# First projection of a two-layer decoder trunk: fewer column sums, unused matmuls between the input loads, a fixed order of TensorE, VectorE and ScalarE, and the state-space parameters behind it

## The chip, the cores and the metric

One core of one Trainium2 chip runs the whole kernel. The metric is the device time of one execution in microseconds (us); below 1 us the text uses the same unit (0.23 us). TensorE (PE) multiplies matrices, VectorE (DVE) and ScalarE (ACT) do elementwise work, GpSimd (POOL) a few small things, and SyncE (SP) issues nearly all the transfers (DMAs). Each engine works through its own list of instructions in order and waits where an operand is not there.

## The reference, cut to what matters

The trunk has two layers; x is 512 tokens by 1024 channels, kept transposed (channels on partitions). Only the start of layer 0 is touched:

```
c_act = silu(c)
mod   = c_act @ ada_w[0] + ada_b[0]           # shift, scale, gate
h     = rms_norm(x, norm_w[0]) * (1 + scale) + shift
u, z  = split(h @ s5_w_in, 2)                 # first projection: 1024 -> 4096 columns
dt = exp(log_dt); mag = exp(lam_re*dt); ab = mag*(cos, sin)(lam_im*dt); q = ...   # state-space parameters
y  = diagonal complex recurrence over u, in chunks of 128 tokens
```

`rms_norm` needs for each token the sum of x*x over 1024 channels, then the power -1/2 of its mean.

## The kernel before

All large products are made of three matmuls on values split in two parts (`fp32r` high part and the rest): high weight by high x, high weight by low x, low weight by high x (`mm3`). A weight tile `wraw` (128x1024) is loaded, ACT copies it to `whi`, DVE subtracts to get `wlo`.

**Before the first matmul.** SP loads c, then x in four loads of two tiles each (`x_sb`), biases, norm weights, constants `cst`, then for k = 0 two tiles of the modulation weights (`adaw`, columns k and 8+k) and one weight tile. PE spreads c over the partitions (L271) and ACT takes its silu (`cact`). ACT squares the eight x tiles, DVE adds them in pairs, and PE sums each pair over the partitions (`col_sums`, L120: four matmuls with one moving column each, sixteen in all) into `pc`. DVE scales `pc` and adds eps, POOL takes the power -1/2 (L129), PE spreads the result over all partitions (`rstd_row`, L134) into `pb`, ACT copies it to `rs`.

**The first projection, u half A (L300 on).** For k = 0..7: two weighted row sums on DVE (`ada_acc`, L103) give shift and scale of 128 channels, two small adds and one small multiply finish them (`ada_fix`, `scale_cols`: `mods`, `acol`). `norm_tile` (L138 to L142) multiplies x by rstd on DVE (`nt`), ACT writes the high part `hhi` and the full value `nh`, DVE subtracts (`hlo`). Then 24 matmuls add into eight accumulators `acc` in PSUM. These 192 matmuls are 'the projection' below. Nothing but a scheduler with priorities sets the order of the engines here.

**After it.** The other 24 column blocks of the projection come as units of 24 matmuls (`unit`, tile `ps_mm`): they fill PE while the recurrence runs. `s5_params` computes the parameters, mostly 128x128 steps on DVE with three kinds of table functions on ACT, and stores powers to DRAM (`wd`). `s5_load` fetches them back (`wt`), with `bB` and the projected `U`; `s5_bl` multiplies on DVE, `s5_mask` on ACT gives `bl`, and `s5_v` multiplies U by bl on PE (`ps_v`, L514). From the first `ps_v` on, sixteen steps of the recurrence run in an order that is written out by hand for PE and DVE; a step begins on DVE with `s5_rot` (`za`, L523), which reads `ps_v`.

Of the kernel before, what the change touches and what calls it, by code (L numbers as in the profile page):

```python
# [41 lines left out]
def hybrid_kernel(ctx: ExitStack, tc: tile.TileContext, a, out, dbg=None):  # L42
# [27 lines left out]
    eps_c, hpi_c, rnd_c = cols[:, 0:1], cols[:, 1:2], cols[:, 2:3]  # L70

# [183 lines left out]
    with tc.tile_pool(name="xa", bufs=1, side="right") as xa, tc.tile_pool(name="psA", bufs=1, space=PSUM) as psA:  # L255
# [10 lines left out]
        SY.dma_start(cst, a["cst"])  # L266
# [3 lines left out]
        for q in range(2):  # L270
            TE.matmul(acc[q], one_row, crow[:, q * T:(q + 1) * T], start=True, stop=True)  # L271
            S.activation(out=cact[:, q * T:(q + 1) * T], in_=acc[q], func=AF.Silu)
# [4 lines left out]
        def mod_cols(k, aw0, aw1, raw):  # L277
            mod_cols.last = ada_acc(k, aw0)
            ada_acc(8 + k, aw1)
            ada_fix(k, 1)  # L280
            ada_fix(8 + k, 1)
            scale_cols(0, k)
            return split_w(raw)

        ld0 = loads(0)

        with tc.high_priority():
            sqs = []
# [10 lines left out]
        for k in range(KT):  # L299
            whi, wlo = mod_cols(k, *loads(k)) if k else w0  # L300
            norm_tile(x_sb[:, k, :], rs if k else pb, acol[:, k:k + 1], mods[:, k:k + 1], hhi[:, k, :], hlo[:, k, :], xa)
            if k == 0:
                acc += [psA.tile([P, T], F32, tag=f"acc{m}", name=f"acc{m}") for m in (6, 7)]
            for m in range(8):
                mm3(acc[m], whi[:, m * P:(m + 1) * P], wlo[:, m * P:(m + 1) * P], hhi[:, k, :], hlo[:, k, :],
                    k == 0, k == KT - 1)
# [1062 lines left out]
```

## Time and profile before

| | |
|---|---|
| runs | 1084.86 us median of 3 (1084.2 to 1087.56) |
| the profiled execution | 1086.08 us, of which the span from first to last instruction is 1084.4 us |
| busy over the span | PE 96%, DVE 71%, ACT 55%, POOL 5% |
| mean granted TensorE clock | 0.992 of full |

Engine busy shares are means over stages with different limits. The rows that matter are those of the first 110 us: when each engine starts a step, how long it takes, and what it waited for before. In a row of the timeline the first number is the start, the second how long the (merged) work lasted, the brackets give the idle time before it and what ended that.

### The profile page before, as it was taken

The page shows a single profiled execution, that of the slowest core. Times are in us where ns is not written, and L with a number is a line of the kernel's source. Part 1 is how long each engine was busy: PE and PEld are TensorE (multiplying, and loading weights), DVE is VectorE, ACT ScalarE, POOL GpSimd, SP SyncE. Part 2 cuts the span into 40 slices and gives each one's busy share as a digit, 9 for nine tenths or more (in the row PEclk, how much of TensorE's full clock was granted, in tenths as well). Part 3 has the DMA queues.
Part 4 walks back from the last instruction along what each step waited for, and adds up shares of the span by engine and source line. Part 5 has one row for each costly group of instructions (what it writes and reads, how often), then busy time and mean ns, then how long its engine had stood idle before and what let it go on. Part 6 is the DMA issues. An engine that isn't in the chain of part 4 may idle for free. (4 is left out here: it accounts for less than half of the span.)

```text
span 1084.4 us, 15225 instructions
## 1 busy us (share of the span) xinstructions
PE 1041.8 (96%) x5620; PEld 869.5 (80%) x5620; DVE 774.9 (71%) x1246; ACT 599.8 (55%) x1163; POOL 57.5 (5%) x62
## 2 busy tenths in 40 slices
PE   7999999998999989999999999999999999999997
PEld 5887878886888868878899777778888888887887
DVE  5994999998999838666785688679951444556253
ACT  4573799989787564334446566733343655424241
POOL 0100000000000000000001004310020000200000
PEclk9999999998999999999999999999999999999999
DMA  8776666675354268866751342132241001123342
GB/s 300 265 244 200 192 195 197 190 214 168 99 148 126 91 248 313 299 208 225 251 179 57 111 164 78 59 99 96 104 131 60 20 20 39 59 72 110 100 146 78
DMA packets 85628, 161.42 MB, mean 149 GB/s; under 512 B 10417, under 2 KB 44593, under 8 KB 85554
## 3 DMA queue, kind: packets, MB, share of 16 engines
q1 hardware_dynamic: 84546, 157.31, 45.0%
q0 software_dynamic: 1008, 3.15, 1.1%
q8 instruction: 44, 0.72, 0.3%
q14 instruction: 30, 0.25, 0.1%
HBM read 141.67 MB, written 18.74 MB: 148 GB/s over the span
## 5 line engine op out<-in xcount | busy, mean ns | idle before, releaser
L79 ACT CAST whi<-wraw 128x1024 fp32r<-128x1024 f32 (+1 forms) x101 | 99.1, 981 | 175.8 <-PE ps_mm L93 74.9
L80 DVE TENSOR_TENSOR wlo<-wraw,whi 128x1024 fp32r<-128x1024 f32 (+1 forms) x101 | 116.1, 1149 | 92.9 <-ACT whi L79 79.6
L92 PE MATMUL ps_mm<-g_hhi,whi 128*128 128x512 f32 x360 | 148.3, 412 | 0.4 <-ACT whi L79 0.4
L93 PE MATMUL ps_mm<-g_hlo,whi 128*128 128x512 f32 x360 | 147.0, 408 | 0.0
L94 PE MATMUL ps_mm<-g_hhi,wlo 128*128 128x512 f32 x360 | 145.8, 405 | 0.5 <-DVE wlo L80 0.5
L94 PEld LDWEIGHTS ps_mm<-g_hhi,wlo 128*128 128x128 f32 x360 | 67.7, 188 | 14.7 <-DVE wlo L80 1.0
L92 PE MATMUL ps_mm<-hhi,whi 128*128 128x512 f32 x192 | 79.3, 413 | 0.0
L92 PEld LDWEIGHTS ps_mm<-g_hhi,whi 128*128 128x128 f32 x360 | 67.7, 188 | 14.3 <-ACT whi L79 0.8
L93 PEld LDWEIGHTS ps_mm<-g_hlo,whi 128*128 128x128 f32 x360 | 67.8, 188 | 12.6
L94 PE MATMUL ps_mm<-hhi,wlo 128*128 128x512 f32 x192 | 75.8, 395 | 0.0
L93 PE MATMUL ps_mm<-hlo,whi 128*128 128x512 f32 x192 | 75.5, 393 | 0.0
L857 DVE SCALAR_TENSOR_TENSOR ac<-ps_mm,cw,ac 128x509 f32<-128x509 f32 (+2 forms) x87 | 64.7, 744 | 3.6 <-ACT ac L854 2.9
L103 DVE SCALAR_TENSOR_TENSOR adaw<-adaw,cact 128x1024 f32<-128x1024 f32 x48 | 58.8, 1228 | 5.0 <-DMA adaw<-in_adaw_dram 4.9
L92 PE MATMUL ps_gh<-yAhi,whi 128*128 128x512 f32 x128 | 53.8, 420 | 3.6 <-ACT yAhi L79 3.6
L346 DVE TENSOR_TENSOR wlo<-wraw,whi 128x1024 fp32r<-128x1024 f32 x40 | 48.7, 1219 | 10.8 <-ACT whi L340 10.8
L340 ACT CAST whi<-wraw 128x1024 fp32r<-128x1024 f32 x40 | 41.8, 1044 | 24.2 <-issue 7.7
L93 PE MATMUL ps_gh<-yAlo,whi 128*128 128x512 f32 x128 | 51.2, 400 | 1.1 <-DVE yAlo L80 1.1
L94 PE MATMUL ps_g<-yBhi,wlo 128*128 128x512 f32 x128 | 50.1, 391 | 1.4 <-DVE wlo L80 1.4
L93 PE MATMUL ps_g<-yBlo,whi 128*128 128x512 f32 x128 | 50.2, 393 | 1.1 <-DVE yBlo L80 1.1
L92 PE MATMUL ps_g<-yBhi,whi 128*128 128x512 f32 x128 | 50.1, 391 | 1.2 <-ACT yBhi L79 1.2
L94 PE MATMUL ps_gh<-yAhi,wlo 128*128 128x512 f32 x128 | 51.0, 399 | 0.0
L94 PEld LDWEIGHTS ps_mm<-hhi,wlo 128*128 128x128 f32 x192 | 36.4, 190 | 8.2
(343 smaller groups left out, 2535.8 us busy)
## 6 DMA issues: line engine op xcount, KB each, us to landing
adaw<-in_adaw_dram SPq DMA_DIRECT2D x48, 512.0 KB
wraw<-in_wginb_dram SPq DMA_DIRECT2D x45, 512.0 KB
wraw<-in_wglu_dram SPq DMA_DIRECT2D x32, 512.0 KB
wraw<-in_winb_dram SPq DMA_DIRECT2D x24, 512.0 KB
bB<-in_bB_dram SPq DMA_DIRECT2D x16, 384.0 KB
wt<-wd SPq DMA_DIRECT2D x48, 128.0 KB
wraw<-in_s5o_a_dram SPq DMA_DIRECT2D x16, 384.0 KB
wraw<-in_wgo_a_dram SPq DMA_DIRECT2D x16, 384.0 KB
```

What stands on the lines that cost most here:

```text
L79: S.copy(hi, src)
L80: V.tensor_tensor(out=lo, in0=src, in1=hi.bitcast(F32), op=ALU.subtract)
L92: TE.matmul(ps, whi, xhi, start=start, stop=False)
L93: TE.matmul(ps, whi, xlo, start=False, stop=False)
L94: TE.matmul(ps, wlo, xhi, start=False, stop=stop)
L103: return V.scalar_tensor_tensor(out=aw, in0=aw, scalar=1.0, in1=cact, op0=ALU.mult, op1=ALU.mult, accum_out=mods[:, n:n + 1]).ins
L340: S.copy(pairs[n][0], raws[n])
L346: V.tensor_tensor(out=lo, in0=raws.pop(n), in1=hi.bitcast(F32), op=ALU.subtract)
L857: V.scalar_tensor_tensor(out=ac[:, d:], in0=ps[:, 0:T - d], scalar=cw[:, n, k:k + 1], in1=ac[:, d:], op0=ALU.mult, op1=ALU.add)
```

## The change

Ahead of the projection: the squares go to eight buffers of their own instead of four that turn, one square is made by DVE, and DVE adds six of the eight into one tile; `col_sums` runs over two tiles instead of four (eight matmuls instead of sixteen). `warm` issues matmuls whose result nobody reads: two on 512 columns and one on 256 of x as it lands, two small ones after the sums, four small ones after `rstd_row`. The scale and eps of `pc` move from DVE to ACT. POOL takes one power of constants at the start (`pw0`). Only 128 of the 514 columns of `cst` are loaded first, the others after k = 1. The copy of the first `whi` goes ahead of the norm, the copy `rs` behind it.

In the projection: PE, DVE and ACT follow the written order (`manual_schedule`). The three passes over the eight accumulators are separate (high, low weight, low x), the two small adds are one (`fix2`), and for each k DVE works in the order row sum, low weight, low x, row sum, add, scale, next `nt`. The parameters are issued after the low part of tile 6.

```diff
+    pw0 = cpool.tile([P, 4], F32, name="pw0")
+    G.tensor_tensor(out=pw0, in0=one1[:, 0:4], in1=mhalf, op=ALU.pow)
...
-        SY.dma_start(cst, a["cst"])
+        SY.dma_start(cst[:, 0:P], a["cst"][:, 0:P])
...
+        def warm(rhs, n=1):
+            for _ in range(n):
+                TE.matmul(acc[5][:, 0:rhs.shape[-1]], one1, rhs, start=True, stop=True)
...
+        def fix2(k):
+            V.tensor_tensor(out=mods[:, k:k + 9:8], in0=mods[:, k:k + 9:8], in1=adab[:, k:k + 9:8], op=ALU.add)
...
+        with tc.high_priority(), tc.manual_schedule(engines={ET.PE, ET.DVE, ET.Activation}):
...
-                if k % 2:
-                    V.tensor_tensor(out=sqs[k], in0=sqs[k - 1], in1=sqs[k], op=ALU.add)
-                    col_sums(sqs[k], 4, pc, k == 1, k == KT - 1)
-            w0 = mod_cols(0, *ld0)
-            rstd_row(rstd_col((), 4, xa, pc, mod_cols.last), 4, pb)
-            rs = xa.tile([P, T], F32, name="rs")
-            S.copy(rs, pb)
+            silu(0)
+            sq(0)
+            sq(1)
+            add(0, 1)
+            warm(x_sb[:, 2, :])
+            sq(2)
+            V.tensor_tensor(out=sqs[3], in0=x_sb[:, 3, :], in1=x_sb[:, 3, :], op=ALU.mult)
+            add(2, 3)
+            add(0, 2)
+            silu(1)
+            warm(x_sb[:, 4, :])
+            sq(4)
+            sq(5)
+            add(4, 5)
+            add(0, 4)
+            sq(6)
+            sq(7)
+            add(6, 7)
+            warm(x_sb[:, 6, 0:256])
+            col_sums(sqs[0], 4, pc, True, False)
+            col_sums(sqs[6], 4, pc, False, True)
+            warm(one1, 2)
+            rc = xa.tile([P, 4], F32, name="rc0")
+            S.activation(out=rc, in_=pc[:, 0:4], func=AF.Identity, scale=1.0 / D, bias=eps_c)
+            G.tensor_tensor(out=rc, in0=rc, in1=mhalf, op=ALU.pow)
+            mod_cols(0, *ld[0][:2])
+            w = get_w(0)
+            rstd_row(rc, 4, pb)
+            warm(one1, 4)
...
+            for k in range(KT):
+                t = norm_nt(k, rs if k else pb)
+                norm_hi(k, t)
+                if k == 0:
+                    S.copy(rs, pb)
+                if k < KT - 1:
+                    ld[k + 1] = loads(k + 1)
+                    ada_acc(k + 1, ld[k + 1][0])
+                V.tensor_tensor(out=w[1], in0=ld[k][2], in1=w[0].bitcast(F32), op=ALU.subtract)
+                lo = norm_lo(k, t)
+                if k == 6:
+                    mod_cols.last = lo
+                for i, (wp, x) in enumerate(((w[0], hhi), (w[1], hhi), (w[0], hlo))):
+                    for m in range(8):
+                        TE.matmul(acc[m], wp[:, m * P:(m + 1) * P], x[:, k, :], start=k == 0 and i == 0,
+                                  stop=k == KT - 1 and i == 2)
+                if k < KT - 1:
+                    ada_acc(9 + k, ld[k + 1][1])
+                    fix2(k + 1)
+                    scale_cols(0, k + 1)
+                    w = get_w(k + 1)
+                if k == 1:
+                    SY.dma_start(cst[:, P:], a["cst"][:, P:])
...
-    s5_params()
+    with tc.issue_after(mod_cols.last):
+        s5_params()
```

Two places of the order are needed below. The first is DVE around tile 7, the last of the projection: `adaw` is a row sum, `nt`, `wlo`, `hlo` belong to the norm and the weights, `p_...` are parameter steps. Before:

```order
L103 SCALAR_TENSOR_TENSOR adaw,mods<-adaw,cact 128x1024
L111 TENSOR_TENSOR mods<-mods,adab 128x1
L138 TENSOR_TENSOR nt<-x_sb,rs 128x512
L111 TENSOR_TENSOR mods<-mods,adab 128x1
L103 SCALAR_TENSOR_TENSOR adaw,mods<-adaw,cact 128x1024
L115 SCALAR_TENSOR_TENSOR acol<-mods,nw 128x1
L80 TENSOR_TENSOR wlo<-wraw,whi 128x1024
L103 SCALAR_TENSOR_TENSOR adaw,mods<-adaw,cact 128x1024
L142 TENSOR_TENSOR hlo<-nh,hhi 128x512
L111 TENSOR_TENSOR mods<-mods,adab 128x1 x2
L218 TENSOR_TENSOR p_798<-p_778 128x128
L115 SCALAR_TENSOR_TENSOR acol<-mods,nw 128x1
```

Now, directly behind the low part of tile 6 and one parameter step:

```order
L201 TENSOR_TENSOR p_781<-p_779 128x128
L221 TENSOR_TENSOR p_799<-p_779 128x128
L205 TENSOR_SCALAR p_781<-p_781 128x128
L222 TENSOR_TENSOR p_799<-p_779 128x128
L206 TENSOR_SCALAR p_781<-p_781 128x128
L223 TENSOR_TENSOR p_799<-p_799 128x128
L207 SCALAR_TENSOR_TENSOR p_787<-p_781 128x128
L224 RECIPROCAL p_799<-p_799 128x128
L208 SCALAR_TENSOR_TENSOR p_787<-p_781,p_787 128x128
L241 MEMSET pw 128x64
L209 TENSOR_SCALAR p_787<-p_787 128x128
L106 SCALAR_TENSOR_TENSOR adaw,mods<-adaw,cact 128x1024
```

Before, both row sums (the second and third `adaw` rows) and the `nt` of tile 7 went ahead of every parameter step. Now the second row sum of tile 7 (L106) follows twelve of them, and its add, its scale and the `nt` come behind it; seven more parameter steps then stand ahead of `wlo` of tile 7.

The second place is PE at the first `ps_v`. Before, after units 0 to 4 (the last is `ps_mm_744`), that is 120 matmuls behind the projection:

```order
L93 MATMUL ps_mm_744<-hlo_93,whi_707 128x512
L94 MATMUL ps_mm_744<-hhi_92,wlo_708 128x512
L514 MATMUL ps_v_896<-U_878,bl_893 128x128 x8
L92 MATMUL ps_mm_949<-hhi_92,whi_741 128x512
L93 MATMUL ps_mm_949<-hlo_93,whi_741 128x512
```

Now, two matmuls before the end of unit 5 (`ps_mm_950`), 142 behind it:

```order
L95 MATMUL ps_mm_950<-hhi_94,whi_742 128x512
L583 MATMUL ps_v_897<-U_879,bl_894 128x128 x8
L96 MATMUL ps_mm_950<-hlo_95,whi_742 128x512
L97 MATMUL ps_mm_950<-hhi_94,wlo_743 128x512
L95 MATMUL ps_mm_1002<-hhi_94,whi_776 128x512
```

So 22 matmuls have moved ahead of the first `ps_v`, and 14 instead of 36 stand between the first and the second. On SP the first load of `bB` moved from ahead of the stores of the projection to behind the three loads of `wt`, and the last of the four `U` loads of the first step stands behind the store of unit 4; before, one went ahead of the store of unit 2 and three between those of units 2 and 3. The load of the raw parameters now goes ahead of those of tiles 6 and 7, before it went behind them.

## Rows read from the trace of the kernel before

**Rows 1.** The page: busy time of the engines, share, instructions.

```profile
PE 1041.8 (96%) x5620; PEld 869.5 (80%) x5620; DVE 774.9 (71%) x1246; ACT 599.8 (55%) x1163; POOL 57.5 (5%) x62
```

**Rows 2.** Timeline of PE, start to second `ps_v`; start us, us, engine, line, operation.

```profile
2.47 3.75 PE L271 MATMUL acc<-crow,one_row 1*128 1x512 f32 x4 [2.47 <-DMA crow<-in_c_dram]
7.06 6.99 PE L120 MATMUL pc<-one,sq 128*128 128x1 f32 x32 [0.84 <-DVE sq L293]
16.38 2.07 PE L134 MATMUL pb<-cst,rc 128*128 128x128 f32 x8 [2.33 <-POOL rc L129]
20.79 3.78 PE L92 MATMUL acc<-hhi,whi 128*128 128x512 f32 x8 [2.33 <-ACT hhi L140]
...
28.21 0.39 PE L94 MATMUL acc<-hhi,wlo 128*128 128x512 f32 x1
...
66.52 0.39 PE L92 MATMUL ps_mm<-hhi,whi 128*128 128x512 f32 x1
...
96.47 3.43 PE L514 MATMUL ps_v<-U,bl 128*128 128x128 f32 x16 [2.59 <-ACT bl L487]
...
109.36 2.05 PE L514 MATMUL ps_v<-U,bl 128*128 128x128 f32 x16 [1.00 <-ACT bl L487]
```

**Rows 3.** Windows, a stretch around the first `ps_v`: busy time, granted clock, DMA.

```profile
97.00:100.00 3.00, 3.00 (x15) 3.00 (x15) 0.06 (x1) 0.83 (x2) 0.00 (x0) 0.50 0.53 153
```

**Rows 4.** Windows, the first eight steps of the recurrence.

```profile
106.00:240.00 134.00, 126.78 (x711) 107.32 (x709) 132.26 (x172) 120.46 (x221) 0.00 (x0) 1.00 0.66 194
```

**Rows 5.** Timeline of all engines ahead of the projection.

```profile
7.83 1.78 SPq L99 DMA_DIRECT2D adaw<-in_adaw_dram  x2
...
9.97 1.32 ACT L291 ACTIVATE sq<-x_sb 128x512 f32<-128x512 f32 x2
...
11.33 0.69 DVE L293 TENSOR_TENSOR sq<-sq 128x512 f32<-128x512 f32 x1 [1.01 <-ACT sq L291]
...
14.24 1.22 DVE L103 SCALAR_TENSOR_TENSOR adaw<-adaw,cact 128x1024 f32<-128x1024 f32 x1
14.32 2.00 POOL L129 TENSOR_TENSOR rc<-rc,mhalf 128x4 f32<-128x4 f32 x1 [13.81 <-DVE mods L111]
...
18.49 0.59 ACT L298 COPY rs<-pb 128x512 f32<-128x512 f32 x1 [7.19 <-PE pb L134]
...
19.11 0.69 DVE L138 TENSOR_TENSOR nt<-x_sb,pb 128x512 f32<-128x512 f32 x1 [3.26 <-ACT rs L298]
...
19.92 0.81 ACT L140 ACTIVATE hhi<-nt,mods,acol 128x512 fp32r<-128x512 f32 x1
```

**Rows 6.** Timeline of PE at 570 us: the same helpers, two columns of tokens.

```profile
569.88 0.50 PE L120 MATMUL pc<-one,sacc 128*128 128x1 f32 x4
...
572.94 0.60 PE L134 MATMUL pb<-cst,rc 128*128 128x128 f32 x4
```

**Rows 7.** Timeline of POOL: a later power of the same shape.

```profile
922.40 1.04 POOL L1170 TENSOR_TENSOR sm<-sm 128x4 f32<-128x4 f32 x1 [129.73 <-DVE sm L1169]
```

**Rows 8.** Timeline of DVE: low parts of tiles 0 and 6, two parameter steps.

```profile
22.59 0.68 DVE L142 TENSOR_TENSOR hlo<-nh,hhi 128x512 fp32r<-128x512 f32 x1
...
53.66 0.68 DVE L142 TENSOR_TENSOR hlo<-nh,hhi 128x512 fp32r<-128x512 f32 x1
...
55.32 0.95 DVE L221 RECIPROCAL p<-p 128x128 f32<-128x128 f32 x1
...
59.42 0.85 DVE L206 TENSOR_SCALAR p<-p 128x128 f32<-128x128 f32 x1
```

**Rows 9.** Timeline of SP and DVE around the first `ps_v`.

```profile
86.78 0.60 SPq L443 DMA_DIRECT2D wt<-wd  x1
...
93.63 0.69 DVE L480 TENSOR_TENSOR tb<-bB,wt 128x512 f32<-128x512 f32 x1 [3.02 <-DMA wt<-wd]
...
99.94 1.23 DVE L523 TENSOR_TENSOR za<-ps_v,tcos 128x1024 f32<-128x1024 f32 x1 [4.89 <-PE ps_v L514]
```

More of the change, by code (lines that the diff above doesn't have):

```diff
@@ L15 @@
 ALU = mybir.AluOpType
+ET = mybir.EngineType
 PSUM = bass.MemoryType.PSUM
@@ L269, in hybrid_kernel @@
         pb = psA.tile([P, T], F32, tag="acc7", name="pb")
-        for q in range(2):
-            TE.matmul(acc[q], one_row, crow[:, q * T:(q + 1) * T], start=True, stop=True)
-            S.activation(out=cact[:, q * T:(q + 1) * T], in_=acc[q], func=AF.Silu)
+        def warm(rhs, n=1):
+            for _ in range(n):
+                TE.matmul(acc[5][:, 0:rhs.shape[-1]], one1, rhs, start=True, stop=True)
         def loads(k):
             return ada_load(k, xa, 5), ada_load(8 + k, xa, 5), load_raw(a["wina"][k])
-        def mod_cols(k, aw0, aw1, raw):
-            mod_cols.last = ada_acc(k, aw0)
+        def fix2(k):
+            V.tensor_tensor(out=mods[:, k:k + 9:8], in0=mods[:, k:k + 9:8], in1=adab[:, k:k + 9:8], op=ALU.add)
@@ L279, in mod_cols @@
+        def mod_cols(k, aw0, aw1):
+            ada_acc(k, aw0)
             ada_acc(8 + k, aw1)
-            ada_fix(k, 1)
-            ada_fix(8 + k, 1)
+            fix2(k)
             scale_cols(0, k)
[L283 to L288, printed above, removed]
-            for k in range(KT):
-                sqs.append(xa.tile([P, T], F32, tag="sq", name="sq", bufs=4))
-                S.activation(out=sqs[k], in_=x_sb[:, k, :], func=AF.Square)
-                if k % 2:
-                    V.tensor_tensor(out=sqs[k], in0=sqs[k - 1], in1=sqs[k], op=ALU.add)
-                    col_sums(sqs[k], 4, pc, k == 1, k == KT - 1)
-            w0 = mod_cols(0, *ld0)
-            rstd_row(rstd_col((), 4, xa, pc, mod_cols.last), 4, pb)
-            rs = xa.tile([P, T], F32, name="rs")
-            S.copy(rs, pb)
@@ L299, in hybrid_kernel, with norm_nt @@
[L299 to L306, printed above, removed]
+        def norm_nt(k, rstd):
+            t = xa.tile([P, T], F32, tag="nt", name="nt", bufs=2)
+            V.tensor_tensor(out=t, in0=x_sb[:, k, :], in1=rstd, op=ALU.mult)
+            return t, xa.tile([P, T], F32, tag="nh", name="nh", bufs=2)
@@ new lines, in norm_hi, with norm_lo, get_w @@
+        def norm_hi(k, th):
+            for o in (hhi[:, k, :], th[1]):
+                S.activation(out=o, in_=th[0], func=AF.Identity, scale=acol[:, k:k + 1], bias=mods[:, k:k + 1])
+        def norm_lo(k, th):
+            return V.tensor_tensor(out=hlo[:, k, :], in0=th[1], in1=hhi[:, k, :].bitcast(F32), op=ALU.subtract).ins
+        def get_w(k):
+            w = [wst.tile([P, 1024], F32R, tag=t, name=t) for t in ("whi", "wlo")]
+            S.copy(w[0], ld[k][2])
+            return w
+        ld = {0: loads(0)}
@@ new lines, in hybrid_kernel, with silu, sq, add @@
+        with tc.high_priority(), tc.manual_schedule(engines={ET.PE, ET.DVE, ET.Activation}):
+            sqs = [xa.tile([P, T], F32, name=f"sq{k}") for k in range(KT)]
+            def silu(q):
+                S.activation(out=cact[:, q * T:(q + 1) * T], in_=acc[q], func=AF.Silu)
+            def sq(k):
+                S.activation(out=sqs[k], in_=x_sb[:, k, :], func=AF.Square)
+            def add(i, j):
+                V.tensor_tensor(out=sqs[i], in0=sqs[i], in1=sqs[j], op=ALU.add)
+            for q in range(2):
+                TE.matmul(acc[q], one_row, crow[:, q * T:(q + 1) * T], start=True, stop=True)
+            silu(0)
[27 more added lines that the diff above has]
+            warm(one1, 4)
+            rs = xa.tile([P, T], F32, name="rs")
+            acc += [psA.tile([P, T], F32, tag=f"acc{m}", name=f"acc{m}") for m in (6, 7)]
+            for k in range(KT):
+                t = norm_nt(k, rs if k else pb)
[20 more added lines that the diff above has]
+                    SY.dma_start(cst[:, P:], a["cst"][:, P:])
```

## The prediction, written before the changed kernel ran

> **What bounds the kernel now.** I read the page first: PE is busy for 96% of the span [rows 1], so idle PE time is scarce and nearly all of it must be looked for by place. Next the timeline of PE over the first 110 us [rows 2]. The reader is to see three things. Ahead of the projection PE does little and waits: its first useful matmul starts at 20.79 us. From 20.79 to 28.21 us 23 matmuls take 7.42 us; from 28.21 to 66.52 us 169 take 38.31, which is 0.2267 each. The eight first ones take about twice that, so they run at the lower of the two clock levels (1.2 and 2.4 GHz), although the column of the granted clock shows full speed there; I go by the durations. The 23 lose 7.42 - 23 x 0.2267 = 2.2 us by it. And from 66.52 us PE runs gapless into the first `ps_v` at 96.47 us, waits 2.59 us for `bl` there, and the granted clock stands at 0.50 from 97 to 100 us [rows 3], so this `ps_v` takes 3.43 us where the next takes 2.05 [rows 2].
>
> Then the windows behind it: from 106 to 240 us DVE is busy 132.26 of 134 us, PE 126.78 [rows 4]. There DVE sets the pace, and its first step of the recurrence, `za`, starts when the first `ps_v` ends. So the time of the whole kernel hangs on that end. The question is how much earlier it comes.
>
> **Ahead of the projection.** t0 is the start of the first `nt` (19.11 us before).
> - The last pair of x tiles lands at about 9.25 us: the second `adaw` issue waits for it and ends at 7.83 + 1.78 [rows 5]. That stays. Before, ACT squared this pair only at 9.97 us, having first waited for one of four buffers; with eight it starts at 9.3. The row of the sum starts 1.36 us behind that of the squares (11.33 - 9.97) and lasts 0.69: ready at 11.35 instead of 12.02.
> - Column sums: 16 matmuls become 8 (32 records become 16). The first four run on the other sum, ready at about 10.5. At the high clock four records take 0.50 us, 0.12 apart [rows 6], so eight take 1.0 and the two groups end at 12.5 us, not 14.05. Whether the clock is high is the open point: PE is then busy from 2.47 us nearly without a gap, first with the spread of c, then with the unused matmuls. The trace does not show such a stretch; it shows the rise twice, in the first tile of the projection and behind the first `ps_v`, each time in the midst of dense matmuls. I take high, and the other as a rival.
> - Mean and eps on ACT: the DVE step took 0.24 with its gaps; I take 0.3. Power on POOL: the first takes 2.00 us [rows 5], a later one of the same shape 1.04 [rows 7]. If the first-use cost is what `pw0` takes away, 1.04; bounds 1.04 and 2.00. `pw0` itself runs at 1 to 3 us, when POOL is idle: nothing, and 2.00 at most if it met the power. With gaps it ends at 13.95.
> - `rstd_row`: 0.60 for four records at the high clock [rows 6], so 1.1 for eight instead of 2.07 [rows 2]. t0 = 15.1, 4.0 us earlier. DVE must have finished both row sums by then, from 11.2 on, 2 x 1.2 + 0.3: 13.9. The trace says only that their data lay there at 11.94 and 14.24; if the second comes as late as that, t0 is 15.8.
> - Before, the copy `rs` and the first `whi` stood between `pb` and `hhi` on ACT [rows 5]; now PE starts 0.69 + 0.81 + 0.1 = 1.6 behind t0, at 16.7. `whi` needs its weights by 14.4 or so: 64 KB of `cst` instead of 257 go ahead of them, and the removed bytes cost nothing later.
> - The unused matmuls lie in PE's waits at the high clock: those behind `rstd_row` take about 0.9 us, PE needs its first operand 1.6 later. At the low clock they don't (below).
>
> **In the projection.** The clock loss of 2.2 us goes, so PE alone would end at 16.7 + 192 x 0.2267 = 60.2. But DVE does not follow. Its order is fixed now, and its cycle per tile is what was measured: from `hlo` of tile 0 to that of tile 6 31.07 us [rows 8] with 13 row sums among the work; now 12, so 29.9, and about 30 with the small add and scale in a chain. The first `hlo` ends its turn 3.5 us behind t0, so tile 6 is done at t0 + 33.5. PE needs 5.44 a tile, more than DVE's 5.0, so up to tile 6 DVE gains on it and PE does not wait. Then twelve parameter steps stand ahead of the second row sum of tile 7: a reciprocal and the two-sided clamp at 0.9 each [rows 8], ten small ones at 0.1 to 0.33, in sum 4.2. Row sum, add, scale and `nt` follow with 1.5 + 0.2 ahead of `nt`: t0 + 39.4, and `hhi` of tile 7 is there at t0 + 40.95. PE asks for it at t0 + 1.6 + 168 x 0.2267 = t0 + 39.7. It waits 1.25 us, and 0.25 more for `wlo`, behind seven more parameter steps. The projection ends at t0 + 1.6 + 43.5 + 1.5 = t0 + 46.6 = 61.7 us, 4.8 earlier than 66.52. Tables for the exponential and the sine load on ACT between tiles 5 and 7, ahead of `hhi`; there DVE is later than ACT, so they cost nothing, and 1.3 us each if not.
>
> **The first ps_v.** 142 matmuls now stand between, 32.2 us: 93.9 us, 2.6 earlier than before, although 22 matmuls more are done. `bl` is then no longer what it waits for: the parameter chain starts 5 us earlier, and ACT makes `bl` right behind the copy of unit 4. The last piece of `U` is issued behind the store of that unit, some 2.9 us ahead of `ps_v`. A landing of about 3 us costs 0.2 (nothing in the trace times this load; bounds 0 and, by the slowest neighbour, 4, see the rivals). Behind the store that waits for unit 4 SP holds only this load and those of the next step, which DVE needs some 7 us after `ps_v`. It lasts 2.05 us at the high clock: end at 96.2 instead of 99.9. Gain 3.65 us. The 22 matmuls moved ahead leave 14 between the two `ps_v`; PE then waits some 6 us at the second for DVE. That costs nothing, as DVE has the same steps in between, but the clock will fall there.
>
> Behind this point the order of all engines is as before, and DVE carries the shift on. 1086.08 us of the profiled execution (span 1084.4 and 1.7 around it) less 3.65 is 1082.4. Its time is 1.2 above the median of the runs, 1084.86, so a median of runs should be 1081.2.
>
> **A rule against it.** The first power ran from 14.32 to 16.32 while DVE did a row sum on two inputs from 14.24 to 15.46 [rows 5]; the later one had no such neighbour [rows 7]. The Trainium skill (SBUF — State Buffer, "Who interferes with whom") says that a VectorE instruction with two inputs in SBUF and a GpSimd instruction that reads SBUF exclude each other, the one that comes second waiting for the whole of the first. The rows fit this as well as a first-use cost: 16.32 - 15.46 leaves 0.86.
>
> **Rivals.**
> - POOL waits for DVE. If the 2.00 us are a wait for the row sum, `pw0` gives nothing: the power then starts at 12.9 beside the second row sum (12.3 to 13.5), ends at 13.5 + 0.86 = 14.4, and t0 is 15.5. Gain 3.2, 1081.6 us.
> - PE does not wait at tile 7, because the parameter steps fall into gaps of DVE. For: DVE has 0.3 us a tile to spare against PE. Against: that is in sum 2 us, and the steps follow in one run. Gain 3.65 + 1.5: 1079.7 us.
> - The clock stays low up to the projection. For: the spread of c was dense for 3.75 us and the column sums behind it still ran at 6.99 / 32 = 0.22 us a record [rows 2], against 0.12 at full speed [rows 6]. Then the unused matmuls take 3.75 / 2 = 1.9 us each on 512 columns and hold the column sums up until 14.9, the power ends at 16.3, `rstd_row` at 18.4, and the four behind it (1.9) end at 20.3, where the projection starts with the old loss of 2.2. PE reaches `ps_v` at 98.2 and ends it at 100.45, 0.55 later than before: 1085.4 us.
> - It gets slower, by the last `U` load. Its place is the wait at the first `ps_v`, which the 22 matmuls have put at the end of the chain. The third `wt` load was issued at 86.78 and used at 93.63 [rows 9], nearly 7 us. If `U` takes that long, PE waits 4, the clock falls and `ps_v` takes 3.43: 1.6 us later than before, 1086.5. From 5.5 us of landing time on it is slower; each further us adds one. Against: few transfers are under way by then.
>
> **How the numbers follow.** Chances: the forecast 0.44 (its own range 1080.2 to 1082.3), POOL waiting 0.14, no wait at tile 7 0.14, low clock 0.18, late U 0.10. What this kernel's measurement can tell from no change is 0.3%, here 3.25 us, so faster means below 1081.6. The forecast is there in six to seven tenths of its share (0.28), POOL waiting in half (0.07), no wait in all: faster 0.49. Slower by as much needs U at 8 us or more, or several us of waits in the new order: 0.08. The rest, 0.43, is no change, most of it on the fast side. The range 1078.6 to 1085.8 leaves out the late U and the far end of the fast side.
>
> **What would show it.** Right: first `nt` near 15 us and the first projection matmul near 16.7, eight matmuls 0.23 apart from the start, a PE wait of 1 to 2 us for `hhi` or `wlo` of tile 7, the projection's end near 61.7, `za` near 96.2, a long wait at the second `ps_v`. The power's duration and the DVE row beside it tell the first rival; matmul spacing at 10 to 17 us the clock. Wrong: waits of PE within tiles 1 to 6, a wait of more than 1 us at the first `ps_v`, or a shift of `za` that DVE does not carry to 240 us.

## The result: slower, and where the time went

The changed kernel takes 1096.47 us (median of 12 runs, 1090.4 to 1101.43) against 1086.56 us of the kernel before (12 runs, 1082.45 to 1090.03): a ratio of 1.009, 95% interval 1.0068 to 1.0112. The forecast was 1081.2 us with a range up to 1085.8, some 3.65 us less than before: wrong in sign. The profiled execution of after took 1096.86 us, span 1095.1.

The page of after, the rows of busy time and of the granted clock by slices:

```profile
PE 1055.2 (96%) x5622; PEld 870.2 (79%) x5622; DVE 776.1 (71%) x1240; ACT 600.6 (55%) x1163; POOL 57.6 (5%) x63
...
PEclk9998999999999999999999999999998999999999
```

Against [rows 1] PE is busy for 13.4 us more, with two more matmul records. DVE and ACT are as before. So the loss is not a new wait: PE's own work has become longer.

The start, which the change is about, went nearly as forecast. PE of after, from the start to behind the first `ps_v` (columns as in [rows 2]):

```profile
2.33 3.75 PE L321 MATMUL acc<-crow,one_row 1*128 1x512 f32 x4 [2.33 <-DMA crow<-in_c_dram]
6.32 4.63 PE L276 MATMUL acc<-x_sb,one 128*128 128x512 f32 x6 [0.24 <-DMA x_sb<-in_xp_dram]
10.74 2.23 PE L123 MATMUL pc<-one,sq 128*128 128x1 f32 x16
...
14.43 1.61 PE L137 MATMUL pb<-cst,rc 128*128 128x128 f32 x8 [0.90 <-POOL rc L346]
...
17.67 2.44 PE L367 MATMUL acc<-hhi,whi 128*128 128x512 f32 x8
19.95 2.03 PE L367 MATMUL acc<-hhi,wlo 128*128 128x512 f32 x8
21.82 2.03 PE L367 MATMUL acc<-hlo,whi 128*128 128x512 f32 x8
...
62.88 0.40 PE L95 MATMUL ps_mm<-hhi,whi 128*128 128x512 f32 x1
...
98.09 2.02 PE L583 MATMUL ps_v<-U,bl 128*128 128x128 f32 x16 [1.91 <-DMA U<-ud]
...
105.02 0.79 PE L97 MATMUL ps_mm<-hhi,wlo 128*128 128x512 f32 x1 [3.99 <-DVE wlo L415]
```

The first matmul of the projection starts at 17.67 us instead of 20.79 [rows 2], and the eight that took 3.78 us there take 2.44. From 17.67 to 62.88 PE never waits. And yet the projection ends only 3.64 us earlier (62.88 against 66.52), and from 21.82 to 62.88 us 176 matmuls start 0.2333 us apart, where [rows 2] gave 0.2267. At `ps_v` the clock stays up, other than in [rows 3]:

```profile
97.00:100.00 3.00, 1.91 (x17) 1.95 (x18) 0.00 (x0) 0.05 (x1) 0.00 (x0) 1.00 0.69 125
```

SP and DVE of after around the first `ps_v`, the counterpart of [rows 9]:

```profile
84.92 0.58 SPq L515 DMA_DIRECT2D bB<-in_bB_dram  x1
...
92.45 0.34 SPq L178 DMA_DIRECT2D ud<-u  x1
92.84 0.43 SPq L518 DMA_DIRECT2D U<-ud  x1
...
93.66 0.69 DVE L548 TENSOR_TENSOR ta<-bB,wt 128x512 f32<-128x512 f32 x1 [5.66 <-DMA bB<-in_bB_dram]
...
100.15 1.23 DVE L592 TENSOR_TENSOR za<-ps_v,tcos 128x1024 f32<-128x1024 f32 x1 [4.47 <-PE ps_v L583]
```

`bB` is issued at 84.92 and lands at 93.66; the last piece of `U` is issued at 92.84 and `ps_v` waits 1.91 us for it. `za` starts at 100.15, not at 99.94 [rows 9]: the gain of the start is gone here. Two things are thus to be explained, this and the loss behind it, and the next table, of three profiled executions, shows them. e1, an experiment told below, is the changed kernel with the operands of all these products at their old addresses. The stages are starts of PE's rows, `za` of DVE's; `ps_y`, `ps_tr` and `f` are products further on in the kernel and serve as marks.

| start of | before | after | shift | e1 | shift |
|---|---|---|---|---|---|
| first matmul of the projection | 20.79 | 17.67 | -3.12 | 17.97 | -2.82 |
| first `ps_mm` (the projection's end) | 66.52 | 62.88 | -3.64 | 61.64 | -4.88 |
| `za`, first step | 99.94 | 100.15 | +0.21 | 98.32 | -1.62 |
| last `ps_y` of the recurrence | 383.97 | 384.96 | +0.99 | 380.90 | -3.07 |
| first `ps_tr` of layer 1 | 716.34 | 721.34 | +5.00 | 713.37 | -2.97 |
| first `ps_y` of layer 1 | 847.37 | 858.19 | +10.82 | 847.33 | -0.04 |
| first `f` | 982.40 | 993.84 | +11.44 | 982.36 | -0.04 |
| the end (span) | 1084.4 | 1095.1 | +10.7 | 1083.5 | -0.9 |

Against before, after loses nearly all of its time behind 385 us, in code that the change doesn't touch (against e1 it has lost 4.1 us by then and 7.5 behind it). Part of the two steps to the first `ps_y` of layer 1 is the clock. Windows from 800 to 860 us of before and of after (the last columns are granted clock, DMA share, GB/s):

```profile
800.00:860.00 60.00, 60.00 (x682) 49.54 (x681) 18.54 (x27) 28.64 (x61) 0.00 (x0) 1.00 0.14 45
```

```profile
800.00:860.00 60.00, 60.00 (x659) 48.86 (x657) 16.14 (x17) 23.33 (x37) 0.00 (x0) 0.91 0.23 67
```

PE is busy for all of both stretches. This fall is in 12 of the 18 profiles of this study, in the old order (4 of 8) and in the new one (8 of 10; e1: 0.94), so neither order is needed for it. Whether the new one makes it more frequent is left open below. The other part is in the spacing of the matmuls. PE of after at 436 us, where two products alternate:

```profile
435.69 0.39 PE L95 MATMUL o<-gH,whi 128*128 128x512 f32 x1
435.92 0.39 PE L96 MATMUL o<-p,whi 128*128 128x512 f32 x1
436.15 0.39 PE L97 MATMUL o<-gH,wlo 128*128 128x512 f32 x1
436.37 0.40 PE L95 MATMUL ps_g<-yBhi,whi 128*128 128x512 f32 x1
...
438.47 0.40 PE L95 MATMUL ps_g<-yBhi,whi 128*128 128x512 f32 x1
```

From 435.69 to 436.37 three matmuls of `o` take 0.2267 each; the nine `ps_g` from 436.37 to 438.47 take 0.2333. Both have 512 columns, the same types and the same clock. What sets them apart is where their moving operand lies in SBUF, the on-chip memory of the operands. By the addresses of the built programs (bytes within a partition), the new tile `pw0` in the constants' pool (16 bytes a partition, 32 taken) pushes all that lies behind it on the left side of SBUF up by 32 bytes: the weights `whi` (32000 to 32032) and `wlo`, and `gH` and `vgh`. The tiles on the right side (`hhi`, `yAhi`, `yBhi`, `g_hhi` at 196352, and their low parts) stay. The products with the moving operand on the right are slow, `o` and `f` with theirs on the left, moved along with the weights, are not. Right-hand ones are 192 matmuls of the first projection, 576 `ps_mm`, 384 `ps_gh`, 384 `ps_g` and 1080 `ps_mm` on `g_hhi`. The last two groups stand behind 385 us: 1464 x (0.2333 - 0.2267) = 9.8 us at most. In the trace of before not every matmul of them follows after 0.2267; by the mean spacings of the two traces (0.2331 and 0.2330 in after, 0.2270 and 0.2285 in before, gaps above 0.26 left out) it is 7.1 us.

### The profile page after: what moved, and what is told of

It is laid out like the page before. It is cut to its first block, busy times and chain, and to the rows that moved or that the text cites. A ratio compares the mean times of both kernels' runs of the same rounds, so it can differ in the third digit from the quotient of the medians.

```text
span 1095.1 us, 15220 instructions
## 1 busy us (share of the span) xinstructions
PE 1055.2 (96%) x5622; PEld 870.2 (79%) x5622; DVE 776.1 (71%) x1240; ACT 600.6 (55%) x1163; POOL 57.6 (5%) x63
## 5 line engine op out<-in xcount | busy, mean ns | idle before, releaser
L82 ACT CAST whi<-wraw 128x1024 fp32r<-128x1024 f32 (+1 forms) x93 | 90.7, 975 | 168.5 <-PE ps_mm L96 77.3
L83 DVE TENSOR_TENSOR wlo<-wraw,whi 128x1024 fp32r<-128x1024 f32 (+1 forms) x93 | 106.4, 1145 | 95.0 <-ACT whi L82 81.9
L95 PE MATMUL ps_mm<-g_hhi,whi 128*128 128x512 f32 x360 | 151.2, 420 | 0.1
L96 PE MATMUL ps_mm<-g_hlo,whi 128*128 128x512 f32 x360 | 150.0, 417 | 0.0
L97 PE MATMUL ps_mm<-g_hhi,wlo 128*128 128x512 f32 x360 | 148.5, 412 | 0.5 <-DVE wlo L83 0.5
L106 DVE SCALAR_TENSOR_TENSOR adaw<-adaw,cact 128x1024 f32<-128x1024 f32 x48 | 58.9, 1229 | 6.3 <-DMA adaw<-in_adaw_dram 6.3
```

What stands on the lines that cost most here:

```text
L82: S.copy(hi, src)
L83: V.tensor_tensor(out=lo, in0=src, in1=hi.bitcast(F32), op=ALU.subtract)
L95: TE.matmul(ps, whi, xhi, start=start, stop=False)
L96: TE.matmul(ps, whi, xlo, start=False, stop=False)
L97: TE.matmul(ps, wlo, xhi, start=False, stop=stop)
L106: return V.scalar_tensor_tensor(out=aw, in0=aw, scalar=1.0, in1=cact, op0=ALU.mult, op1=ALU.mult, accum_out=mods[:, n:n + 1]).ins
```

## The experiments

The theories on record bear these names. DISTANCE: the spacing goes by the distance in SBUF between the weights and the moving operand. PLACE: it goes by the place of one of them alone. Against both stands that the new order itself slows PE. For the gain that is missing at `ps_v`: LOADS (the next step's loads are issued too late, and issuing them earlier brings it), QUEUE (what is moved ahead on SP holds up the weight loads behind it) and SP ORDER (the loads are late only for what stands ahead of them on SP). Each ratio is to the kernel before on the same chip. e6 and e7 were run once and are judged by the spacing; the time of one run can't tell a difference of one per cent.

**e1: the changed kernel at the old addresses.** `pw0` goes into the unused half of the 32 bytes of `mhalf`, so that the weights and the moving operands lie as before the change. (Only tiles of the start, such as `x_sb` and `adaw`, lie elsewhere: the change enlarges their pool.)

```diff
-    mhalf = cpool.tile([P, 4], F32, name="mhalf")
+    mh = cpool.tile([P, 8], F32, name="mhalf")
+    mhalf, pw0 = mh[:, 0:4], mh[:, 4:8]
...
-    pw0 = cpool.tile([P, 4], F32, name="pw0")
```

> The changed kernel, with the output of the early power put into the unused half of the 32 bytes that hold `mhalf`, so that every tile stands at the address it had before the change. Theory ADDRESS (the 32 bytes that the new tile `pw0` takes move all tiles on the left side of SBUF, the weights `whi` and `wlo` among them, against the moving operands `hhi`, `yAhi`, `yBhi`, `g_hhi` on the right side, and matmuls of 512 columns then follow each other 0.2333 us apart instead of 0.2267): spacing 0.2267 in every stage, as before the change. The time falls by 12 to 15 us from 1096.5, to 1081 to 1085, and the clock does not fall between 800 and 860 us. Theory ORDER (the three separate passes of the projection and the fixed order cost the time, or the chip ran slower on that day): spacing stays at 0.2333 and the time at 1096.

Measured: 1086.78 us, ratio 0.9993 (0.9971 to 1.0014), and 0.2267 is the commonest spacing of every product again. The loss is gone with one tile's place. The median is not as low as the 1081 to 1085 expected, and against the expectation the clock falls from 800 to 860 us (0.94). The row of `ps_g` in e1 (mean ns of one behind the busy time; 397 in after, see e16):

```profile
L95 PE MATMUL ps_g<-yBhi,whi 128*128 128x512 f32 x128 | 50.1, 392 | 1.2 <-ACT yBhi L82 1.2
```

**e2: the kernel before with a tile of 16 bytes that nobody uses.**

```diff
     eps_c, hpi_c, rnd_c = cols[:, 0:1], cols[:, 1:2], cols[:, 2:3]
+    cpool.tile([P, 4], F32, name="pad")
```

> The kernel before, with one unused tile of 16 bytes per partition behind the last constants, which takes 32 bytes and shifts the left side of SBUF as the change does; no instruction is added or removed. ADDRESS: spacing 0.2333 in all products whose moving operand is on the right side (`hhi`, `yAhi`, `yBhi`, `g_hhi`), 0.2267 where both operands are on the left (`gH`, `vgh`); time 1094 to 1100, ratio to before 1.008 to 1.013. ORDER: no difference, ratio 1.000 within 0.002.

Measured: 1094.19 us, 1.0077 (1.0049 to 1.0104), 0.2333 for the products with the moving operand on the right and 0.2267 for the others. The old order loses the same: the loss needs none of the rest of the change.

**e3: the changed kernel, its right side moved down by 32 bytes.** A pad `RPAD` on the right is in the kernel already.

```diff
-RPAD = 56
+RPAD = 64
```

> The changed kernel, with the padding at the end of the right side 64 instead of 56 elements wide: the right side moves down by 32 bytes. Weights and moving operands then stand to each other as before the change modulo 64 bytes, but both at 32 modulo 64. ADDRESS in its relative form (the distance of the two operands counts): spacing 0.2267, time 1081 to 1085. ADDRESS in its absolute form (the weights' own address counts): spacing 0.2333, 1096. ORDER: 1096.

Measured: 1095.09 us, 1.0073 (1.0048 to 1.0098), 0.2333. I had thought that a distance changed by 64 would do; it does not.

**e4: the kernel before, its left side moved by 64 bytes** (the pad of e2 with 16 columns in place of 4).

> The kernel before, with an unused tile of 64 bytes per partition behind the last constants. If only the distance modulo 64 bytes counts, spacing stays 0.2267 and the ratio to before is 1.000 within 0.002. If any shift between the sides slows the matmuls, spacing is 0.2333 or more and the ratio 1.008 to 1.013. ORDER: no difference.

Measured: 1094.77 us, 1.0079 (1.0048 to 1.0109), 0.2333. It agrees with e3.

**e5: the changed kernel, its right side moved up by 32 bytes** (`RPAD = 48`). Distances are as before, addresses on both sides are not.

> The changed kernel, with the padding at the end of the right side 48 instead of 56 elements wide: the right side moves up by 32 bytes, as the left side did, so weights and moving operands are exactly as far apart as before the change (164352 bytes from `whi` to `hhi`), though every address differs by 32. Theory DISTANCE (what counts is how far the weights and the moving operand are apart): spacing 0.2267 and 1083 to 1088 us, as with the same addresses. Theory PLACE (what counts is the place of each operand in its own 64 or 128 bytes): spacing 0.2333 and 1094 to 1097.

Measured: 1092.02 us, 1.0013 (0.999 to 1.0037), 0.2267. DISTANCE holds, PLACE fell.

**e6 and e7: the kernel before, its left side moved by 128 and by 256 bytes.**

> The kernel before, the left side shifted by 128 bytes. Shifts of 32 and 64 gave 0.2333. DISTANCE with a period of 128 bytes: spacing back at 0.2267. With a period of 256, 512 or more, or with one good distance alone: 0.2333.

> The kernel before, the left side shifted by 256 bytes. Period of 128 or 256 bytes: 0.2267. Period of 512 (the weights of one matmul are 512 bytes long, and before the change the distance is a multiple of 512) or more: 0.2333.

Measured: 0.2333 at 128 bytes (one run of 1094.71 us), 0.2267 at 256 (1087.38). From weights to `hhi` it was 164352 bytes before, 642 x 256; from `whi` to `gH` and `vgh` 49152, 192 x 256. Of the shifts tried, 0 and 256 are fast; 32, 64 and 128 are slow.

**e16: the kernel before, a tile of 16 bytes behind the weights' pool.** Weights and right side stay, `gH` and `vgh` move by 32.

```diff
     rpad.tile([P, RPAD], F32, name="rpad")
+    padp = ctx.enter_context(tc.tile_pool(name="padp", bufs=1))
+    padp.tile([P, 4], F32, name="pad")
```

> The kernel before, with the 32 bytes behind the weights' pool instead of ahead of it: `whi` and `wlo` keep their place against `hhi`, `yAhi`, `yBhi` and `g_hhi` on the right; what shifts is all the rest of the left side, with `gH` and `vgh`, the moving operands of the other two products. Theory DISTANCE of the pair weights and moving operand: 0.2267 where it was slow (the first projection, `ps_mm`, `ps_gh`, `ps_g`) and 0.2333 in the products `o` (from 410 to 555 us) and `f` (from 982 to 1049), which the other shifts left at 0.2267. 288 matmuls of each kind cost 1.9 us each by it: the time rises by 2 to 4 us, ratio 1.001 to 1.005. If the distance is between the moving operand and anything else on the left: 0.2333 in the first group as well, ratio 1.007 to 1.01.

Measured: 1092.7 us, 1.0033 (1.0008 to 1.0057). The two groups change places. Groups of instructions by line (mean ns of one behind the busy time), two of after and the same two of e16:

```profile
L95 PE MATMUL ps_g<-yBhi,whi 128*128 128x512 f32 x128 | 50.9, 397 | 1.2 <-ACT yBhi L82 1.2
...
L96 PE MATMUL f<-vgl,whi 128*128 128x512 f32 x96 | 37.5, 390 | 0.5 <-DVE vgl L83 0.5
```

```profile
L94 PE MATMUL ps_g<-yBhi,whi 128*128 128x512 f32 x128 | 50.2, 392 | 1.2 <-ACT yBhi L81 1.2
...
L95 PE MATMUL f<-vgl,whi 128*128 128x512 f32 x96 | 38.0, 396 | 0.5 <-DVE vgl L82 0.5
```

A slow one shows 396 to 397 ns, a fast one 390 to 392 (the matmuls overlap, so the mean is longer than the spacing). In e16 `o` and `f` are slow, 2 x 288 matmuls: 576 x 0.0067 = 3.8 us by count, 3.6 us by the ratio. So it is the pair of weights and moving operand that counts, for every product of this kernel.

**e12: e1 once more**, on the chip of e9 to e11.

> The changed kernel with the addresses of before once more, unchanged, beside the others on one chip: the profile before had no fall of the clock between 800 and 860 us, most later ones have. Theory ADDRESS with a gain of some 1.5 us in the first stage: ratio 0.997 to 1.000, and again a fall of the clock by 3 us in that stretch. If the change gives nothing at all: 1.000 to 1.002.

Measured: 1087.01 us, 0.9999 (0.9979 to 1.0019). In both runs of e1 the forecast's ratio, 1 - 3.65 / 1086 = 0.9966, lies below the interval. So the forecast gain is missing for a second reason, apart from the addresses, and the following experiments ask where. First e1's own rows, PE from the projection's end, with SP, DVE and ACT:

```profile
61.64 0.39 PE L95 MATMUL ps_mm<-hhi,whi 128*128 128x512 f32 x1
...
83.46 0.58 SPq L515 DMA_DIRECT2D bB<-in_bB_dram  x1
...
91.03 0.30 SPq L518 DMA_DIRECT2D U<-ud  x1
...
92.33 0.69 DVE L548 TENSOR_TENSOR ta<-bB,wt 128x512 f32<-128x512 f32 x1 [5.44 <-DMA bB<-in_bB_dram]
...
94.39 1.33 ACT L556 ACTIVATE bl<-ta,cst 128x512 f32<-128x512 f32 x2 [4.00 <-DVE ta L550]
...
96.26 2.02 PE L583 MATMUL ps_v<-U,bl 128*128 128x128 f32 x16 [2.27 <-DMA U<-ud]
...
98.32 1.22 DVE L592 TENSOR_TENSOR za<-ps_v,tcos 128x1024 f32<-128x1024 f32 x1 [3.96 <-PE ps_v L583]
```

and the `ps_v` of e12:

```profile
96.16 3.65 PE L583 MATMUL ps_v<-U,bl 128*128 128x128 f32 x16 [2.30 <-DMA U<-ud]
```

PE is there at 96.26 - 2.27 = 93.99 and waits for `U`, which lands 5.2 us behind its issue. `bB` is issued at 83.46, where before it went at 60.42, and lands at 92.33; `bl`, made from it, is complete at 94.39 + 1.33 = 95.72, so PE would have waited some 1.7 us with `U` in time. After the same wait `ps_v` takes 2.02 us in one execution and 3.65 in the other: the clock falls in one of them. `za` starts at 98.32 and 99.85. With the old order six profiles have it between 96.59 (e16) and 99.94, so one profile shows no gain at `za`. The row of e16:

```profile
96.59 1.23 DVE L525 TENSOR_TENSOR za<-ps_v,tcos 128x1024 f32<-128x1024 f32 x1 [3.51 <-PE ps_v L516]
```

**e8: `bB` first, parameters and the first step's loads with high priority** (in e1).

```diff
+    s5_bB(steps[0])
     fill(40)
-    with tc.issue_after(mod_cols.last):
+    with tc.issue_after(mod_cols.last), tc.high_priority():
         s5_params()
...
-    cur = s5_load(0)
+    with tc.high_priority():
+        cur = s5_load(0)
```

> The changed kernel with the addresses of before, and the loads of the first step of the recurrence earlier: `bB` ahead of the eight stores of the projection, the parameters and the rest of the step's loads (`wt`, `U`) with high priority. By that 120 instead of 142 matmuls stand between the projection and the first `ps_v`. Theory LOADS (with the addresses restored the forecast gain is missing at the first `ps_v` because `bB` and the last `U` were issued behind stores and landed at 92.3 and 96.3 us): the first `ps_v` starts at 88.5 to 91 us instead of 96.26, with a wait of less than 1 us, `za` at 91 to 93 instead of 98.3, and the stage of the recurrence ends 3 to 7 us earlier; the time falls by 2 to 6 us against the run with the same addresses. Theory QUEUE (SP waits at the parameters' stores and holds up the weights behind them): PE waits for `whi` or `wlo` between 62 and 90 us, and `za` gains under 2 us.

Measured: 1087.71 us, 0.9983 (0.9965 to 1.0001). SP works off twelve stores `wd` from 70.69 to 77.36 in one piece, and the weights behind them (`wraw`, issued at 77.46) are late: PE waits 3.38 us at 82.51 and 1.16 at 84.40 for them. That is what QUEUE said, and `za` at 98.43 gains nothing against e1.

**e9: only the first step's loads with high priority** (in e1), and **e11, the same line in the kernel before.**

```diff
-    cur = s5_load(0)
+    with tc.high_priority():
+        cur = s5_load(0)
```

> The changed kernel with the addresses of before, and one line more: the loads of the first step (`wt`, `bB`, `U`) have high priority, the parameters have not. SP then issues `bB` ahead of the eight stores of the projection, `U` behind the fourth of them, and `wt` right behind the last parameter store; the weights are not held up. 138 instead of 142 matmuls stand ahead of the first `ps_v`. Theory LOADS (what keeps the gain of the projection from the first `ps_v` is where SP issues the loads of the first step): PE comes to `ps_v` at 61.7 + 138 x 0.2267 = 93 us and waits less than 1 us, `za` starts at 95 to 96.5 instead of 98.3, and the time is 2 to 3 us below that with the same addresses. Theory DMA (the engines of the DMA are full there, so that another order only makes something else late): `za` not before 97.5, time as with the same addresses.

> The kernel before with that one line alone. LOADS: the projection ends at 66.5, 132 matmuls follow, so PE comes to `ps_v` at 96.4 at the earliest and waits little; `za` at 98.4 to 99, where the runs of the old order had 98.1 to 99.9: no change in time (ratio 0.998 to 1.001). If the line gives as much here as in the changed kernel, the projection has nothing to do with it.

Measured: e9 1091.47 us, 1.0049 (1.0028 to 1.0069); e11 1093.16 us, 1.0064 (1.0045 to 1.0083). `za` starts at 102.39 in e9 and at 104.00 in e11, not at 95 to 96.5 and 98.4 to 99. LOADS fell, and the old order loses by the same line too. SP, DVE and PE of e9:

```profile
65.87 1.76 SPq L518 DMA_DIRECT2D U<-ud  x4
...
80.67 2.82 SPq L253 DMA_DIRECT2D wd<-p  x6
...
85.83 2.06 SPq L512 DMA_DIRECT2D wt<-wd  x3
...
94.60 0.69 DVE L549 TENSOR_TENSOR tb<-bB,wt 128x512 f32<-128x512 f32 x1 [3.86 <-DMA wt<-wd]
...
98.57 3.78 PE L583 MATMUL ps_v<-U,bl 128*128 128x128 f32 x16 [5.48 <-ACT bl L556]
```

`U` goes early now and no longer counts, but it has to wait on SP for the projection's stores and with it all that stands behind: the last `wd` ends at 83.5, `wt` lands at 94.6, and `ps_v` waits 5.48 us for `bl`.

**e10: the parameters no longer tied behind the low part of tile 6** (in e1: `with tc.issue_after(mod_cols.last)` left out).

> The changed kernel with the addresses of before, without the edge that holds the parameters back to the low part of tile 6. Theory LOADS: PE still waits for `bl` or `U` at the first `ps_v` (`bB` is issued behind the stores as before), though all of `U` now goes ahead of the store of unit 4, so up to 2 us less: `za` at 96 to 98.5, time as with the same addresses within 2 us. A rival (the edge is what brought the gain of the projection): the projection ends 1 us later or more, and the time rises by as much.

Measured: 1089.29 us, 1.0016 (0.9998 to 1.0033). `bB` still lands at 93.29, `ps_v` waits 3.51 us for `bl` and starts at 96.73, `za` at 100.36, later than the 96 to 98.5 expected. The tie is not what holds it up.

**e13: the first step's `bB` and `U` issued by POOL** (in e1), and **e15, the same in the kernel before.**

```diff
-        SY.dma_start(s.bB, ...)
+        q = SY if i else G
+        q.dma_start(s.bB, ...)
...
-            SY.dma_start(s.U[32 * j:32 * j + 32], ...)
+            q.dma_start(s.U[32 * j:32 * j + 32], ...)
```

> The changed kernel with the addresses of before; the first step's `bB` and `U` are issued by POOL, which is idle there, instead of SP: `bB` some 20 us into the kernel, `U` as soon as the projection's store has landed. 121 instead of 142 matmuls stand ahead of the first `ps_v`. Theory SP ORDER (the loads are late because SP issues them behind waiting stores): only `wt` is left, issued near 82 and landed by 89 to 90, `bl` at 92 to 93.5, `za` at 94.5 to 97 instead of 98.3 to 99.9, and the time 2 to 4 us below that with the same addresses, ratio to before 0.996 to 0.998. Theory DMA FULL (what is late is the sum of the transfers): `wt` lands at 92 or later and `za` is at 98 or later, ratio 0.999 to 1.002.

> The kernel before with `bB` and `U` of the first step issued by POOL. Here `wt` was what the first step waited for, so SP ORDER expects `za` at 97.5 to 99.5 (before: 98.1 to 99.9) and a ratio of 0.998 to 1.001. If it gains as much as the changed kernel with the same edit, the early end of the projection is worth nothing.

Measured: e13 1087.01 us, 0.9999 (0.998 to 1.0019); e15 1092.51 us, 1.0041 (1.0027 to 1.0055). POOL, DVE and PE of e13:

```profile
59.81 0.93 POOL L516 DMA_DIRECT2D bB<-in_bB_dram  x1
68.69 2.22 POOL L519 DMA_DIRECT2D U<-ud  x4 [7.95 <-DMA ud<-p]
...
91.18 0.69 DVE L550 TENSOR_TENSOR tb<-bB,wt 128x512 f32<-128x512 f32 x1 [2.58 <-DMA wt<-wd]
...
94.02 2.89 PE L584 MATMUL ps_v<-U,bl 128*128 128x128 f32 x16 [3.91 <-ACT bl L557]
...
96.95 1.22 DVE L593 TENSOR_TENSOR za<-ps_v,tcos 128x1024 f32<-128x1024 f32 x1 [4.35 <-PE ps_v L584]
```

With both loads off SP the trace does what SP ORDER said: `wt` (issued 82.31) is the last to land, `za` starts 3.0 us earlier than in [rows 9] (but only as early as in e16, with the old order), and this execution took 1081.04 us, the fastest of its twelve (the others 1082.74 to 1092.13). The median shows nothing of it. In e15 `wt` is the last to land as well, and `za` is at 101.72, later than the 97.5 to 99.5 expected.

**e14: only `U` with high priority** (in e1; `U` is taken out of `s5_load` and issued by itself).

```diff
     cur = s5_load(0)
+    with tc.high_priority():
+        s5_U(cur)
```

> The changed kernel with the addresses of before; of the first step's loads only `U` has high priority, so that SP issues it behind the fourth store of the projection. `wt` and `bB` stand as they did. By the rows, `bl` would be there at 95.7 anyway, so SP ORDER and DMA FULL both expect little: PE waits for `bl` instead of `U`, `za` within 1 us of 98.3, ratio 0.998 to 1.001. If `za` comes 2 us earlier, `U` alone was late.

Measured: 1096.39 us, 1.007 (1.0052 to 1.0088). SP, DVE and PE:

```profile
66.32 1.76 SPq L528 DMA_DIRECT2D U<-ud  x4
...
75.99 1.41 SPq L253 DMA_DIRECT2D wd<-p  x3
...
90.08 0.58 SPq L523 DMA_DIRECT2D bB<-in_bB_dram  x1
...
98.17 0.69 DVE L557 TENSOR_TENSOR ta<-bB,wt 128x512 f32<-128x512 f32 x1 [6.33 <-DMA bB<-in_bB_dram]
...
105.43 1.23 DVE L601 TENSOR_TENSOR za<-ps_v,tcos 128x1024 f32<-128x1024 f32 x1 [5.24 <-PE ps_v L592]
```

The loads of `U` stop SP until the projection's stores have landed (66.32), the first `wd` goes at 75.99 instead of 67.01 in e1, `bB` at 90.08 instead of 83.46: `za` is 7.1 us later than in e1, where a shift of at most 1 us was expected. In this kernel a load that waits in SP's list holds up all that stands behind it.

No kernel of this study is faster than the one before by more than its interval.

## Why the prediction was wrong, step by step

**The step that failed: "`pw0` itself runs at 1 to 3 us, when POOL is idle: nothing".** The instruction costs nothing that the rows show; its tile costs 8 to 11 us (e2 1.0077 and e4 1.0079 of 1086 are 8.4 and 8.6; after to e1, 1.009 / 0.9993, is 10.5), beside 7.1 to 9.8 by count behind 385 us alone. I asked for the time of each new instruction and never where its result is put and what moves with it. No rival had it: the range ended at 1085.8, and the one rival that got slower, by the last `U`, was another mechanism.

**Ahead of the projection** the forecast held but for 1 us: first `nt` at 16.08 (said 15.1), first matmul 17.67 (16.7). The column sums took 2.23 us, not 1.0, and `rstd_row` 1.61 (in e1 2.07), not 1.1: the granted clock was 0.83 from 13 to 16 us (in e1 0.62 from 13 to 17), so the rival of the low clock held in part. POOL of after, then POOL and DVE of e1:

```profile
1.18 1.01 POOL L73 TENSOR_TENSOR pw<-one,mhalf 128x4 f32<-128x4 f32 x1 [0.67 <-DVE cols L68]
13.35 1.02 POOL L346 TENSOR_TENSOR rc<-rc,mhalf 128x4 f32<-128x4 f32 x1 [11.16 <-DVE adaw L106]
```

```profile
12.12 1.22 DVE L106 SCALAR_TENSOR_TENSOR adaw<-adaw,cact 128x1024 f32<-128x1024 f32 x1
...
12.89 1.32 POOL L346 TENSOR_TENSOR rc<-rc,mhalf 128x4 f32<-128x4 f32 x1 [10.70 <-ACT rc L345]
```

The first use costs 1.01 us, no more than a later one. In e1 the power begins beside a row sum that ends at 13.34 and is done 0.87 us behind it (14.21), in [rows 5] 0.86; in after its operand comes at 13.27, the row sum ends at 13.29, and the power takes 1.02. The rival that POOL waits for DVE was right, at a price of about 0.3 us in e1, and no row shows the first-use cost that I took as the forecast's ground. The Trainium skill (SBUF — State Buffer, "Who interferes with whom") has a GpSimd instruction that reads SBUF wait for a VectorE one with two SBUF inputs that started first. The rows of before and of e1 agree with it.

**In the projection.** "The clock loss of 2.2 us goes": 0.4 of it stays in after (2.44 for the first eight, 2.03 later), 0.1 in e1 (61.64 - 17.97 - 192 x 0.2267). The wait of 1.25 + 0.25 us at tile 7 did not come: the rival without it was right, PE finds each operand of tile 7 there in time, so the parameter steps had room. A start 1.3 us late (17.97) and no wait make 61.64 in e1 where 61.7 was said: right by two misses that cancel. In after the spacing adds 192 x 0.0067 = 1.3.

**The first `ps_v`.** PE arrives at 93.99 in e1 (said 93.9). "A landing of about 3 us costs 0.2": it was 5.2 us and cost 2.3, which is the mechanism of the late-`U` rival at a part of its price. "`bl` is then no longer what it waits for" failed too: in e1 it is complete 1.7 us behind PE's arrival, and where `U` is early (e9, e10, e13) PE waits 3.5 to 5.5 us for `bl`, whose `bB` or `wt` lands late. The long wait at the second `ps_v` did not come: PE waited 3.99 us for `wlo` ahead of it, at 105.02 in after. "Behind this point the order of all engines is as before" was true of PE and DVE and not of SP: the order that I quoted myself has `bB` moved behind `wt`, and I priced only `U`.

**"DVE carries the shift on" held.** In the thirteen profiles with the old spacing in the recurrence the last `ps_y` starts 282.4 to 284.2 us behind `za`, wherever `za` starts, from 96.59 (e16) to 105.43 (e14). That keeps a shift to within 1.8 us. What the forecast had no term for is the clock behind it. From the last `ps_y` to the first one of layer 1 it takes 463.4 us in before, 463.7 in e11 and 462.2 in e13, but 466.4 in e1, which loses its lead of 3 us there, and 470.3 in e12, which has a second such fall at 560 to 580 us (0.91). Windows of e1, then of e13:

```profile
820.00:840.00 20.00, 20.00 (x222) 16.31 (x220) 3.78 (x4) 6.27 (x10) 0.00 (x0) 0.83 0.18 54
```

```profile
820.00:840.00 20.00, 20.00 (x216) 16.32 (x214) 4.89 (x4) 8.40 (x13) 0.00 (x0) 1.00 0.13 46
```

**What stays open.** What the medians lose is shown for single executions only, as each kernel has one trace. Their granted clock points to the same place: over all executions its mean is 0.987 in e1 against 0.991 in the kernel before on the same chip (e12: 0.986 against 0.991; e13: 0.987 against 0.990). The three of e1 at 0.984 or less took 1088.9 us in the mean, the three at 0.990 or more 1083.9; by that, 0.004 of clock is an estimated 3 us, about what is missing. But the clock also falls after a wait ([rows 3]), so it can follow a loss as well as make one; two edits of the old order (e11 and e15, both with a late `za`) are at 0.987 too. No run separates whether the new order brings the lower clock. And why the distance counts is not shown: only that it does.

## What to carry to other kernels

Where a tile is added, compare the addresses of the matmul operands before and after: 32 bytes in a pool of constants cost this kernel 0.8 to 1.0%, more than the edit was forecast to win; a change should be measured once with its new tile in space that was there already. If PE is busy for longer with the same matmuls, compare their spacing, product by product, before looking for waits. Work brought forward on PE is a gain only if the loads of the next stage come forward too, and here moving one load up in SP's list (e9, e14) only held up others. And a gain of a few us has to be looked for stage by stage in several traces: one stretch at a lower clock hides it.

## What the runs showed of the hardware

- A 512-column matmul of this kernel follows the last one after 0.2267 us where the addresses of weights and moving operand lie as before or are moved against each other by 256 bytes, after 0.2333 where they are moved by 32, 64 or 128 (2.9%). The Trainium skill (SBUF — State Buffer, "Who interferes with whom") gives PE one read port for the moving operand and one for the weights and calls them independent. By the measured spacing the place of one operand against the other counts all the same, and the measurement decides; what couples them is not shown.
- After a wait of 2.3 us at `ps_v` the clock fell in one execution (3.65 us for it, e12) and not in another (2.02, e1).
- With PE busy throughout, the granted clock from 820 to 840 us was 1.00 in some executions (before, e13) and 0.83 in others (e1, e12). The stage from the last `ps_y` to the first one of layer 1 took 462.2 to 463.7 us in the executions with full clock there (before, e11, e13), 466.4 with this fall (e1).
- Loads took 5.2 us (`U`, e1) to 8.9 (`bB`, e1: 83.46 to 92.33) from issue to the use that waited for them.
